# Sample attention of branches A and B: scores of block n + 1 and values of block n - 1 emitted as one task

## The chip, the cores and the metric

The kernel runs on one core of a Trainium2 chip. The metric is the device time of one execution in microseconds (us). The time before is 1967.59 us, the median of 3 runs (1961.37 to 1970.36).

The engines are named as in the profile: PE is TensorE's matrix multiply, PEld its weight load, DVE is VectorE, ACT is ScalarE, POOL is GpSimd, SP is SyncE, which here only issues DMAs.

## The reference, cut to what matters

One layer of a streaming encoder works on 1152 tokens: 1024 of a prompt and 8 samples of 16 new tokens each. Three attention branches are computed from one projection, each is multiplied by a gate, and their projections are summed; a feed-forward part follows.

```
x += W_o( sum_b sigmoid(gate_b(xn)) * P_b(branch_b(xn)) ),  xn = RMSNorm(x)
x += W_down( relu(RMSNorm(x) W_up)^2 )
```

The change touches the attention of the samples in branches A (band attention with a bias by distance) and B (forgetting attention). For each of the 8 samples, 16 queries of 8 heads read 512 cached keys and 16 new ones:

```
kk = jnp.concatenate([k_cache, k_new], axis=1)
vv = jnp.concatenate([v_cache, v_new], axis=1)
s = jnp.einsum('bqhd,bkhd->bhqk', q, kk).astype(jnp.float32) * (d ** -0.5)
s = s + rel_bias_lookup(rel_bias, dist)
p = jax.nn.softmax(s, axis=-1).astype(vv.dtype)
o = jnp.einsum('bhqk,bkhd->bqhd', p, vv)
```

## The kernel before, in words

**Stages.** After the projections come six attention stages, in this order: the prompt in branch A, the samples in A, the prompt in B, the samples in B, the prompt against the memory, the samples against the memory (`attend`, L1851). Then a rest of filler work, the output projection and the feed-forward part.

**What sets the order.** In the attention stages the order of the instructions is written by a planner, `Plan` (L58), while the program is built. It keeps modelled times of its own for each engine and each load. Its list of tasks is the stage's: scores, transposes, values and turns. Each task has a `ready` function, an `emit` function and the name of a chain; of one chain, tasks go in order, and a chain's first task that isn't ready holds the others of that chain back, though not those of another. `run` (L148) looks at up to 12 tasks and emits the first whose `ready` has passed. If there is none, `fill` (L135) emits one step of the filler instead: three matmuls of 128x384 with the result `z`. The filler is one stream for all stages, first the gates' products (`gates`, L948) and then the products of the merge (`merge`, L1005). The merge goes through the branches in the order A, B, memory, and through three thirds of the tokens. The planner's choice fixes each engine's order; on the chip each engine then goes through its instructions in that order and waits where data are late.

**The merge's operands.** A third of a branch's output is loaded in four quarters, each to a staging buffer `wst` (a ring of 3) and then split in a high and a low part, `hi` (`load`, L1043). For branch A a third may load once the last gate products of that third are emitted, for branch B once A's last merge product of that third is emitted.

**One sample in A and B** (`sample_ab`, L1509). A block n is one sample. Eight heads with 16 queries each fill 128 rows of scores as four groups of 32, so the scores (L1576) and the values (L1638) are matmuls on a 128x32 part of the array, placed by `tile_position`: 4 for the cached keys (`kd`) with 512 columns and 4 for the new keys (`kn`) with 16, and 20 with 128 columns for the values (`vd` and the new ones). After the scores, `soften` adds the bias and takes the maximum on DVE, then comes the exponential on ACT and the normalization on POOL or DVE (`exp_norm`). Five transposes (L1611) bring the weights into the form that the values need, ACT copies them to `spt`, the values follow, ACT copies the result to `of`, and a transpose of it (`turn`, L1662) ends the block. All transposes and the filler use the whole 128x128 array. The task loop (L1683) lists, per n: transposes of n - 1, scores of n, turn of n - 2, values of n - 1.

**The loads of a sample** are issued on SP's queue: keys (`kd`, 1 MB in A and B, a ring of 3, `KB`), values (`vd`, 1 MB, ring of 3) and, in B, a bias per block. Key n is issued once the scores of n - 3 are emitted, value n once the values of n - 3 are.

**The samples against the memory** (`sample_m`, L1693) are not touched by the change. They are 4 pairs of samples with keys and values of 512 KB (`kd<-in_cmk`, `vd<-in_cmv`) and the same steps; a score matmul there is 32x256. `queries` fills `qb`, which the scores read.

Most helpers' instructions carry line L203, all matmuls through the `pe` helper L215 and transposes L222.

Of the kernel before, what the change touches and what calls it, by code (L numbers as in the profile page):

```python
# [31 lines left out]
DB = 8  # L32
# [155 lines left out]
def tile_encoder(ctx: ExitStack, tc: tile.TileContext, i, o):  # L188
# [40 lines left out]
    def tl(pool, shape, dt=F32, tag=None, bufs=None):  # L229
        uid[0] += 1  # L230
        return pool.tile(list(shape), dt, tag=tag, name=f"{tag}_{uid[0]}", **({"bufs": bufs} if bufs else {}))
# [501 lines left out]
    for k in range(KD):  # L733
        n = {0: 1, 1: 1, 2: 1, 3: 1, 4: 2, 6: 2}.get(k)
# [270 lines left out]
    def merge(wpool, late):  # L1005
# [104 lines left out]
        for bi, (f, c) in ((bi, st) for bi in range(3) for st in steps):  # L1110
            x = 8 * bi + f
            for k in range(4):
                yield lambda: max(at["w", x], at["o", order[bi], c, k], plan.bank("z") if k == 0 else 0.0)
                if k == 0:
# [4 lines left out]
                    for y in {(4, 0): (2, 3), (5, 0): (3,), (6, 0): (), (7, 0): (), (7, 2): (2,)}.get((f, c), (2,) if c == 0 else ()):  # L1119
                        if x + y < 24:  # L1120
# [5 lines left out]
        late["h"] = lambda: (([[hi[c, kh] for kh in range(2)] for c in range(NC)],  # L1126
                              [[lo[c, f] for f in range(8)] for c in range(NC)]), order[2] == "m")

    def exp_norm(p, s, n, nm, pool, scale=-1.0, sm=None):

        sm = tl(pool, (P, 1), tag="sm", bufs=4)
        act.activation(p, s, AF.Exp, bias=nm, scale=scale, accum_out=sm)
        yield plan.op("act", n + 240)
        ri = tl(pool, (P, 1), tag="ri", bufs=4)
        vec.reciprocal(ri, sm)
        yield plan.op("vec", 8)
        k = plan.first(n, ("vec2", 0.3), ("gps1", 0))
        (vec if k == "vec2" else gps).tensor_scalar(p, p, ri, 1.0, ALU.mult, ALU.mult)
        yield plan.op(k, n)
# [369 lines left out]
    def sample_ab(b, pool):  # L1509
# [66 lines left out]
        def scores(n):  # L1576

            cols_ = (0, PAST), (PAST, DS)

            def soften(st):  # L1580
                yield plan.now + plan.LAT
                s = tl(pool, (P, NK), tag="s")
                bias, nm = biases[n if b == "b" else 0], None
                for (bk, ps), (x, hn) in zip(st, cols_):
                    m = tl(pool, (P, 1), tag="nm", bufs=4)
                    vec.tensor_tensor_reduce(s[:, x:x + hn], ps[:, :hn], bias[:, x:x + hn], -1.0,
                                             BIG if nm is None else nm, ALU.add, ALU.min, m)
                    t = plan.op("vec", hn)
                    plan.free(bk, t)
                    nm = m  # L1590
                at["m", n] = 0
                yield t
                yield from exp_norm(s, s, NK, nm, pool)
                ss_[n] = s
                at["p", n] = plan.t

            def ready():
                return max(at["k", n], at["q"], plan.bank("s"), 0 if n < 2 else at["t", n - 2])

            def emit():  # L1600
                st = []
                for x, hn in cols_:
                    st.append((plan.take("s"), tl(psum["s"], (P, 512), tag="s")))
                    for pr in range(4):
                        pe.matmul(st[-1][1][32 * pr:32 * pr + 32, :hn], qb[:, n, pr, :],
                                  kn[:, pr, n * DS:(n + 1) * DS] if x else kk[n][:, pr, :], start=True, stop=True, tile_position=(0, 32 * pr))
                at["s", n] = 0
                plan.spawn(soften(st))
            return [(ready, emit, ("s", n))]

        def transposes(n):  # L1611

# [25 lines left out]
        def values(n):  # L1638

            def ready():  # L1640
                return max(at["T", n, 512], at["T", n, P], at["V", n], plan.bank("tp"))

            def emit():
                bk = plan.take("tp")
                pv = tl(psum["tp"], (P, 512), tag="tp")
                for k in range(5):
                    for pr in range(4):
                        pe.matmul(pv[32 * pr:32 * pr + 32, 0:P], pts[n][k][:, 32 * pr:32 * pr + 32], vv[n][k][:, pr * P:(pr + 1) * P],
                                  start=k == 0, stop=k == 4, tile_position=(0, 32 * pr))
                at["v", n] = 0  # L1650
                plan.spawn(take(bk, pv[:, 0:P], n))
            return [(ready, emit, ("v", n))]

        def take(bk, pv, n):
            yield plan.now + plan.LAT
            of[n] = tl(pool, (P, P), tag="of")
            act.activation(of[n], pv, AF.Copy)
            t = plan.op("act", P)
            plan.free(bk, t)
            at["o", n] = t  # L1660
# [19 lines left out]

        plan.spawn(keys())
        plan.spawn(vals())
        for n in range(DB + 2):  # L1683
            if 0 <= n - 1 < DB:
                yield from transposes(n - 1)
            if n < DB:
                yield from scores(n)
            if 0 <= n - 2:
                yield from turn(n - 2)
            if 0 <= n - 1 < DB:  # L1690
                yield from values(n - 1)

    def sample_m(pool):  # L1693
# [165 lines left out]
    with tc.tile_pool(reuse_waits="tile", name="fg", bufs=1, side="right") as pool:  # L1859
        plan.spawn(forget_gates(pool))  # L1860
        attend("aa", lambda p: prompt_ab("a", p))
    attend("sa", lambda p: sample_ab("a", p))
    late["a"] = 0
    attend("ab", lambda p: prompt_ab("b", p))
# [451 lines left out]
```

## Time and profile before

| What | Value |
|---|---|
| profiled execution | 1967.87 us |
| its span | 1966.1 us |
| median of the runs shown | 1967.59 us (1961.37 to 1970.36) |
| mean granted clock of TensorE | 0.996 |
| samples in A, samples in B (about) | 566 to 645 us, 850 to 936 us |
| prompt against memory, samples against memory (about) | 936 to 1019 us, 1019 to 1066 us |

The profiled execution's own time is 0.28 us above the median of the runs, and its span is what the trace covers. A row of the timeline gives the start in us, the duration in us, the engine, the line, the operation, the tiles (out <- in), the part of the array or of the tile that it works on, its size, its type and the count of records merged in it; in brackets stands the idle time just before and what ended it. A matmul of full float32 on a part of the array shows two records, so four of them are x8; one of 128x384 shows one. A row of the windows gives start and end, length, then busy time and count for PE, PEld, DVE, ACT and POOL, the granted clock of TensorE as a share of full speed, the busy share of the DMA engines, and GB/s.

### The profile page before, as it was taken

The numbers are of one execution on the slowest core, as the hardware profiler recorded it, in microseconds if no ns is written. First come the engines' busy times: TensorE is split into PE (matmuls) and PEld (weight loads), VectorE is DVE, ScalarE is ACT, GpSimd is POOL, SyncE is SP. The second block draws the span as 40 slices with busy tenths as digits, with TensorE's granted clock in tenths as the row PEclk, the third lists the DMA queues.
The fourth block names the chain that finished last, engine by engine and source line by source line (L and its number), as shares of the span: only waits on it lengthen the run. The fifth ranks groups of instructions, "written<-read, shape, count | busy, mean of one in ns | idle before, by whom it ended". The sixth has DMA issues, their size and how long they took to land. (4 is left out here: it accounts for less than half of the span.)

```text
span 1966.1 us, 33787 instructions
## 1 busy us (share of the span) xinstructions
PE 1931.2 (98%) x12338; PEld 1704.0 (87%) x12338; DVE 1210.7 (62%) x2305; ACT 947.8 (48%) x1846; POOL 531.5 (27%) x575
## 2 busy tenths in 40 slices
PE   9999999999999999999999999999999999999999
PEld 9887888788888888888998987899999997888887
DVE  7866657675633555523675824975565565785775
ACT  7645556556643556533452314554444453543332
POOL 4243433342210334211133101254445430000000
PEclk9999999999999999999999999999999999999999
DMA  8456454743267433188667442054343459563463
GB/s 279 159 160 183 122 169 150 251 124 105 84 207 277 158 107 101 62 280 293 196 223 267 150 163 97 22 198 151 132 144 125 141 190 325 174 204 96 134 194 127
DMA packets 203812, 330.52 MB, mean 168 GB/s; under 512 B 29285, under 2 KB 101622, under 8 KB 199550
## 3 DMA queue, kind: packets, MB, share of 16 engines
q1 hardware_dynamic: 146504, 270.44, 42.2%
q10 hardware_dynamic: 57142, 57.93, 8.9%
q8 instruction: 97, 1.59, 0.3%
q14 instruction: 69, 0.57, 0.1%
HBM read 243.11 MB, written 85.18 MB: 167 GB/s over the span
## 5 line engine op out<-in xcount | busy, mean ns | idle before, releaser
L1912 PE MATMUL b<-r 128*128 128x512 f32 (+2 forms) x2200 | 456.5, 356 | 4.7 <-ACT r L203 2.7
L1912 PEld LDWEIGHTS b<-r 128*128 128x128 f32 x2200 | 378.9, 189 | 62.7 <-ACT r L203 3.6
L203 ACT ACTIVATE r<-fa 128x512 fp32r<-128x512 f32 (+4 forms) x264 | 213.0, 816 | 336.3 <-PE b L1912 284.3
L203 DVE TENSOR_TENSOR r<-fa,r 128x512 fp32r<-128x512 f32 (+4 forms) x264 | 268.2, 1028 | 145.3 <-ACT r L203 138.8
L215 PE MATMUL z<-hi,whi 128*128 128x384 f32 x960 | 313.4, 359 | 2.7 <-DVE tg L203 2.6
L1912 PE MATMUL b<-r,r 128*128 128x320 f32 (+1 forms) x1928 | 287.8, 299 | 5.7 <-DVE r L203 5.6
L1912 PEld LDWEIGHTS b<-r,r 128*128 128x128 f32 x1928 | 271.0, 190 | 7.4 <-DVE r L203 7.4
L215 PE MATMUL z<-hi,wlo 128*128 128x384 f32 x768 | 259.6, 338 | 0.0
L203 POOL TENSOR_TENSOR fa<-fa 128x512 f32<-128x512 f32 x114 | 173.3, 1528 | 225.0 <-ACT fa L203 125.8
L215 PE MATMUL z<-wa,hi 128*128 128x512 f32 (+1 forms) x732 | 199.4, 359 | 5.8 <-ACT wa L203 2.8
L215 PE MATMUL z<-lo,whi 128*128 128x384 f32 x576 | 194.9, 338 | 0.0
L215 PEld LDWEIGHTS z<-hi,whi 128*128 128x128 f32 x960 | 177.3, 189 | 16.7 <-issue 8.0
L203 ACT ACTIVATE s<-s,nm 128x256 f32<-128x256 f32 (+8 forms) x180 | 121.2, 679 | 63.8 <-DVE nm L203 61.0
L215 PEld LDWEIGHTS z<-wa,hi 128*128 128x128 f32 x732 | 126.3, 188 | 25.4 <-ACT wa L203 3.6
L215 PEld LDWEIGHTS z<-hi,wlo 128*128 128x128 f32 x768 | 145.0, 189 | 0.0
L203 POOL TENSOR_SCALAR s<-s,ri 128x256 f32<-128x256 f32 (+7 forms) x107 | 73.7, 693 | 232.2 <-DVE ri L203 223.6
L215 PE MATMUL z<-wa,lo 128*128 128x512 f32 (+1 forms) x366 | 129.0, 354 | 0.0
L203 DVE CUSTOM_DVE_ANT_0 s<-s,bias 128x384 f32<-128x384 f32 (+3 forms) x144 | 74.5, 555 | 88.0 <-PE s L215 87.2
L215 PEld LDWEIGHTS z<-lo,whi 128*128 128x128 f32 x576 | 109.7, 190 | 0.0
L203 DVE TENSOR_TENSOR fa<-b,fa 128x256 f32<-128x256 f32 (+1 forms) x160 | 71.6, 452 | 58.7 <-PE b L1912 52.0
L222 PE MATMUL tp<-ident,s 128*128 128x128 f32 (+1 forms) x680 | 105.7, 277 | 1.2 <-POOL s L203 1.1
L203 ACT ACTIVATE pt<-tp 128x256 f32<-128x256 f32 (+3 forms) x153 | 65.4, 449 | 85.1 <-PE tp L222 79.7
(229 smaller groups left out, 3129.8 us busy)
## 6 DMA issues: line engine op xcount, KB each, us to landing
td<-fa SPq DMA_DIRECT2D x112, 256.0 KB, 2.1
rw<-in_w_in SPq DMA_DIRECT2D x96, 256.0 KB, 3.2
fa<-td SPq DMA_DIRECT2D x80, 256.0 KB, 2.7
fa<-in_w_down SPq DMA_DIRECT2D x76, 256.0 KB, 3.1
fa<-in_w_up SPq DMA_DIRECT2D x32, 512.0 KB, 4.1
tg<-tg ACTq DMA_DIRECT2D x72, 192.0 KB, 2.6
th<-tg SPq DMA_DIRECT2D x72, 192.0 KB, 3.0
wst<-in_w_g ACTq DMA_DIRECT2D x48, 256.0 KB, 3.2
```

Of the source, the lines that this page charges most:

```text
L203: ins = f(*a, **k)
L215: ins = nc.tensor.matmul(out, lhsT, rhs, **k)
L222: ins = nc.tensor.transpose(*a)
L1912: pin(nc.tensor.matmul(ps, lh, rh, **k))
```

## The change

A new function `joined` takes the scores of block n + 1 and the values of block n - 1 and makes one task of them. Its `ready` is the later of both, and its `emit` calls both, the scores first. All score tasks now have the same chain name, `"s"`, in place of one per block, so that joined tasks go in order. The loop lists the scores of blocks 0 and 1 first and then, per n: transposes of n - 1, turn of n - 2, the joined task; the last two blocks' values stand alone. That makes 6 joined tasks in each of A and B. Matmuls, transposes, copies and loads are the same as before in number and size; what moves is their order, in these two stages and, since the planner's modelled times go on from there, in the stages behind them.

```diff
+    def joined(scores, values):
+        if values is None:
+            return scores
+        (r0, e0, chain), (r1, e1, _) = scores, values
+        def emit():
+            e0()
+            e1()
+        return lambda: max(r0(), r1()), emit, chain
...
-            return [(ready, emit, ("s", n))]
+            return [(ready, emit, "s")]
...
         plan.spawn(keys())
         plan.spawn(vals())
-        for n in range(DB + 2):
-            if 0 <= n - 1 < DB:
+        yield from scores(0)
+        yield from scores(1)
+        for n in range(1, DB + 2):
+            if n - 1 < DB:
                 yield from transposes(n - 1)
-            if n < DB:
-                yield from scores(n)
             if 0 <= n - 2:
                 yield from turn(n - 2)
-            if 0 <= n - 1 < DB:
+            if n + 1 < DB:
+                yield joined(*scores(n + 1), *values(n - 1))
+            elif n - 1 < DB:
                 yield from values(n - 1)
```

**Place 1: PE, the samples in A, about the fourth block.** Tiles are named as in the rows: `s` are scores (from keys `kd` or new keys `kn` and queries `qb`), `tp<-vd,spt` are values, `tp<-ident,s` and `tp<-ident,of` transposes, `z` the filler. Before:

```order
L215 MATMUL z_6663<-hi_154_222,wlo_6408 128x384
L215 MATMUL s_6725<-kd_6502,qb_6319 32x512 x4
L215 MATMUL s_6730<-kn_6317,qb_6319 32x16 x4
L215 MATMUL z_6663<-hi_154_222,whi_6407 128x384
L215 MATMUL z_6663<-lo_162_230,whi_6407 128x384
...
L215 MATMUL tp_6748<-vd_6378,spt_6707 32x128 x16
L215 MATMUL tp_6748<-v_1156_6324,t_1152_6320 32x128 x4
L222 MATMUL tp_6777<-ident_203,s_6699 128x128 x4
```

With the change:

```order
L215 MATMUL z_6723<-hi_163_231,wlo_6383 128x384
L215 MATMUL s_6744<-kd_6502,qb_6319 32x512 x4
L215 MATMUL s_6749<-kn_6317,qb_6319 32x16 x4
L215 MATMUL tp_6754<-vd_6378,spt_6704 32x128 x16
L215 MATMUL tp_6754<-v_1156_6324,t_1152_6320 32x128 x4
L222 MATMUL tp_6787<-ident_203,s_6699 128x128 x4
```

Three filler matmuls that stood between the scores and the values stand elsewhere now. Over the whole program, a stretch of PE's order on 32-wide parts of the array, with full-array work on both sides, occurs 10 times in A where it was 15, 9 in B where it was 10, and 7 in the samples against the memory where it was 6.

**Place 2: PE, the end of the samples in B and the start of the prompt against the memory.** The rows `z<-hi,wlo` with `lo` beside them are the last gate products; the first row with a new `hi` after them are merge products. The products of `z_10894` before, of `z_10906` with the change, are the first of the last third of branch A's operand. Before, from the last gate product on:

```order
L215 MATMUL z_10729<-hi_164_232,wlo_10319 128x384
L215 MATMUL z_10808<-hi_2055_10439,whi_10395 128x384
...
L215 MATMUL tp_10838<-vd_10483,spt_10764 32x128 x16
L215 MATMUL tp_10838<-v_1927_9781,t_1925_9779 32x128 x4
...
L215 MATMUL z_10867<-hi_2093_10631,whi_10395 128x384
...
L222 MATMUL tp_10879<-ident_203,of_10865 128x128
...
L215 MATMUL z_10894<-hi_2119_10776,whi_10395 128x384
```

With the change:

```order
L222 MATMUL tp_10791<-ident_203,of_10781 128x128
...
L215 MATMUL z_10741<-hi_164_232,wlo_10324 128x384
L215 MATMUL z_10848<-hi_2065_10467,whi_10378 128x384
...
L215 MATMUL z_10882<-hi_2102_10681,whi_10378 128x384
...
L215 MATMUL z_10906<-hi_2122_10805,whi_10378 128x384
```

In both there are 24 filler matmuls between the last gate product and the last third. The last values of branch B's samples and the turn that followed them stood in between, and now stand ahead of the last gate product.

**Place 3: PE and SP, the samples against the memory, from the first scores on.** `kd` and `vd` are the memory's keys and values here. PE before:

```order
L215 MATMUL s_12015<-kd_11918,qb_11915 32x256 x4
L215 MATMUL s_12015<-kd_11939,qb_11915 32x256 x4
...
L222 MATMUL tp_12071<-ident_203,s_12041 128x128 x2
...
L215 MATMUL s_12092<-kd_11960,qb_11915 32x256 x4
L215 MATMUL s_12092<-kd_11984,qb_11915 32x256 x4
L215 MATMUL tp_12102<-vd_11925,spt_12070 32x128 x8
L215 MATMUL tp_12102<-vd_11949,spt_12070 32x128 x8
...
L222 MATMUL tp_12154<-ident_203,of_12132 128x128 x2
```

PE with the change:

```order
L215 MATMUL s_11923<-kd_11854,qb_11822 32x256 x4
L215 MATMUL z_11945<-hi_2393_11857,whi_11472 128x384
...
L222 MATMUL tp_11958<-ident_203,s_11942 128x128 x2
...
L215 MATMUL tp_11965<-vd_11843,spt_11957 32x128 x8
L215 MATMUL tp_11965<-vd_11875,spt_11957 32x128 x8
L222 MATMUL tp_11988<-ident_203,of_11986 128x128 x2
L215 MATMUL s_11993<-kd_11888,qb_11822 32x256 x4
L215 MATMUL s_11993<-kd_11911,qb_11822 32x256 x4
L222 MATMUL tp_12015<-ident_203,s_12008 128x128 x2
L215 MATMUL tp_12021<-vd_11902,spt_12014 32x128 x8
```

SP's queue with the change, in the same place (before, no `wst` stood between the keys and values here):

```order
L203 DMA kd_11825<-in_cmk 128x1024
L203 DMA vd_11843<-in_cmv 128x1024
L203 DMA th_11849<-tg_76 128x384
L203 DMA kd_11854<-in_cmk 128x1024
L203 DMA wst_11859<-oTb_72 128x384
L203 DMA wst_11868<-oTb_72 128x384
L203 DMA vd_11875<-in_cmv 128x1024
L203 DMA wst_11877<-oTb_72 128x384
...
L203 DMA kd_11888<-in_cmk 128x1024
```

Before, 24 filler matmuls stand between the first scores and their transposes, 9 between these and the next scores and 12 between the first values and their turn. With the change the first scores are followed by 6 filler matmuls up to their transposes and 3 more up to the first values, and from these on, through turn, second scores, second transposes and second values, by none. The filler's next product there, `z_11945`, is the one that reads the operand which the three `wst` loads fill. Between the last matmul of the prompt against the memory and the first scores stand 57 filler matmuls before and 51 with the change.

## The prediction

> **What bounds the kernel now.** First the page's head and its busy times:
>
> ```profile
> span 1966.1 us, 33787 instructions
> PE 1931.2 (98%) x12338; PEld 1704.0 (87%) x12338; DVE 1210.7 (62%) x2305; ACT 947.8 (48%) x1846; POOL 531.5 (27%) x575
> ```
>
> PE works 98% of the span, no other engine over 62%, so the time is PE's work plus the few places where PE waits. Then the windows of the stages concerned, in order the samples in A, the samples in B, the prompt against the memory, the samples against the memory:
>
> ```profile
> 566.00:636.00 70.00, 70.00 (x750) 59.22 (x749) 23.09 (x75) 25.70 (x61) 5.64 (x8) 1.00 0.75 281
> 850.00:936.00 86.00, 82.81 (x819) 72.85 (x818) 27.40 (x82) 30.60 (x72) 11.66 (x19) 0.98 0.88 305
> 936.00:1019.00 83.00, 82.85 (x511) 79.44 (x511) 60.85 (x111) 45.20 (x123) 20.57 (x17) 1.00 0.60 185
> 1019.00:1066.00 47.00, 46.07 (x410) 41.05 (x409) 23.16 (x50) 10.25 (x26) 9.59 (x11) 1.00 0.84 299
> ```
>
> In A PE never waits. In B it is idle for 86.00 - 82.81 = 3.19 us, at a DMA share of 0.88; the two memory stages lose 0.15 and 0.93 us. So the change can win only what a matmul on a part of the array costs beyond its own work and 3 us of waits in B; it can lose more wherever it leaves PE without filler. The waits in B, from PE's timeline, and the window behind the longest:
>
> ```profile
> 863.19 1.06 PE L215 MATMUL s<-kd,qb 128*32 128x512 f32 x8 [0.22 <-DMA kd<-in_cbk]
> 894.69 1.07 PE L215 MATMUL s<-kd,qb 128*32 128x512 f32 x8 [0.96 <-DMA kd<-in_cbk]
> 909.30 0.33 PE L222 MATMUL tp<-ident,of 128*128 128x128 f32 x1 [1.90 <-ACT of L203]
> 910.50:913.90 3.40, 3.40 (x15) 3.23 (x14) 0.01 (x1) 0.40 (x1) 0.72 (x2) 0.51 0.87 335
> ```
>
> Twice the scores wait for keys and once a turn waits for ACT's copy of its values, 0.22 + 0.96 + 1.90 = 3.08 us. After the 1.90 us the granted clock is 0.51 for 3.40 us, which costs 3.40 x 0.49 = 1.7 us more, though PE counts as busy.
>
> **Part 1, fewer visits to a part of the array.** What one costs is read in A, where nothing waits: scores alone, values alone, and a place where both already stand together, each with the filler at its sides.
>
> ```profile
> 596.16 0.34 PE L215 MATMUL z<-hi,wlo 128*128 128x384 f32 x1
> 596.43 1.07 PE L215 MATMUL s<-kd,qb 128*32 128x512 f32 x8
> 597.75 0.34 PE L215 MATMUL z<-lo,whi 128*128 128x384 f32 x1
> ...
> 582.46 0.34 PE L215 MATMUL z<-hi,wlo 128*128 128x384 f32 x1
> 582.73 1.08 PE L215 MATMUL tp<-vd,spt 128*32 128x128 f32 x32
> 584.24 0.34 PE L215 MATMUL z<-lo,whi 128*128 128x384 f32 x1
> ...
> 611.64 0.33 PE L215 MATMUL z<-hi,wlo 128*128 128x384 f32 x1
> 611.90 1.08 PE L215 MATMUL tp<-vd,spt 128*32 128x128 f32 x32
> 613.02 1.04 PE L215 MATMUL s<-kd,qb 128*32 128x512 f32 x8
> 614.32 0.34 PE L215 MATMUL z<-lo,whi 128*128 128x384 f32 x1
> ```
>
> From filler to filler it is 597.75 - 596.16 = 1.59 us around scores, 1.78 around values, 2.68 around both. One filler matmul takes 0.18 of each (three start in 0.53 us, row below), so apart it is 1.41 + 1.60 = 3.01, together 2.50: about 0.5 with all neighbours out, but the filler ahead and behind is itself drawn out by the visit, and counting two spacings (0.35) out, 1.59 + 1.78 - 0.35 - 2.68 = 0.34. I take 0.34; the bounds are 0.34 and 0.5. The order shows 26 visits where there were 31, not 12 fewer, since several already stood together: 5 x 0.34 = **-1.7 us** (bounds -1.7 and -2.5). [...]
>
> **Part 2, samples in A.** The joined task asks for the keys of block n + 1 while the values of n - 1 are due, so keys are needed a few us earlier than when they could drift. The stage has no wait to lose or give back, and filler on both sides: **0**, bounds 0 and +2 (two key waits of B's larger size, 0.96).
>
> **Part 3, samples in B.** Joined, a score whose keys are late holds the values behind it on PE, and with them ACT's `of`, the turn, and the ring slot for the next values. On the other side `of` gets more room, since the turn stands behind more work. I keep the two key waits at two or three times their size, 0.22 + 0.96 to about 3.5, and let the 1.90 and its slow clock go: 3.5 - 4.8 = **-1.3 us**. Bounds: all of it gone, -4.8; a wait of 0.96 at each of the 6 joined tasks on top of what is there and one slow stretch, about +4 net.
>
> **Part 4, start of the prompt against the memory.** After the last gate product PE goes on with merge products of branch A, whose last third is only loaded once that gate product is emitted:
>
> ```profile
> 932.63 0.34 PE L215 MATMUL z<-hi,wlo 128*128 128x384 f32 x1
> 940.85 0.45 PE L215 MATMUL z<-hi,whi 128*128 128x384 f32 x1 [0.15 <-DVE hi L203]
> ```
>
> It takes 940.85 - 932.63 = 8.22 us to the last quarter of that operand, and PE had 0.15 us to wait. With the change the last values and the turn stand ahead of the gate product; 34 matmuls at 0.177 are left, 6.0 us. The load path is the same length, so PE waits 2.2 instead of 0.15: **+2.0 us**. Bounds 0 (the loads are faster with the queue emptier) and +4 (this stage's own keys in their way).
>
> **Part 5, samples against the memory.** This stage isn't edited, but loses its cover: the filler's next product reads an operand whose loads stand between the keys and values on SP's queue, so the planner puts little filler there. Rows of PE, SP, DVE, POOL and ACT before:
>
> ```profile
> 1019.10 0.34 PE L215 MATMUL z<-hi,wlo 128*128 128x384 f32 x1
> 1019.63 0.34 PE L215 MATMUL z<-hi,wlo 128*128 128x384 f32 x1
> 1018.95 0.46 SPq L203 DMA_DIRECT2D kd<-in_cmk  x1
> 1021.64 0.65 SPq L203 DMA_DIRECT2D kd<-in_cmk  x1
> 1030.27 0.33 SPq L203 DMA_DIRECT2D kd<-in_cmk  x1
> 1028.91 0.64 PE L215 MATMUL s<-kd,qb 128*32 128x256 f32 x8
> 1029.87 0.64 PE L215 MATMUL s<-kd,qb 128*32 128x256 f32 x8 [0.32 <-DMA kd<-in_cmk]
> 1034.71 0.38 PE L222 MATMUL tp<-ident,s 128*128 128x128 f32 x2
> 1035.13 0.39 ACT L203 ACTIVATE spt<-tp 128x256 f32<-128x256 f32 x1 [3.47 <-PE tp L222]
> 1037.48 1.06 PE L215 MATMUL tp<-vd,spt 128*32 128x128 f32 x32
> 1037.73 0.43 DVE L203 TENSOR_REDUCE nm<-s 128x1 f32<-128x256 f32 x1 [0.34 <-PE s L215]
> 1039.05 0.48 POOL L203 TENSOR_SCALAR s<-s,ri 128x256 f32<-128x256 f32 x1 [0.80 <-DVE ri L203]
> 1038.65 0.37 ACT L203 ACTIVATE of<-tp 128x256 f32<-128x256 f32 x1
> th<-tg SPq DMA_DIRECT2D x14, 192.0 KB, 6.5
> ```
>
> The durations: three fillers 0.53; keys landed 1029.87 - 1021.64 = 8.2 after their issue, which is 10.9 after the first key's; softmax from the scores' end to POOL's end 1039.53 - 1037.73 = 1.80; transposes to the end of `spt` 0.81; values to the end of `of` 1039.02 - 1037.48 = 1.54. Walk along the new order from the first key's issue at t = 0. 51 fillers take 9.0; first scores at 8.9 to 9.5, their second half waits for its keys until 10.9: **1.4**. Scores end at 11.6, six fillers reach 12.6, softmax is done at 13.4: **0.7**. Transposes to 13.7, three fillers to 14.3, values to 15.3, `of` at 15.8: **0.5**. Turn to 16.2, half of the second scores to 16.8, then the fourth keys: issued 11.3 after the first, landed 6.5 (as the smaller `th`, last row) to 8.2 later, t = 17.8 to 19.5; I take 18.7: **1.9**. Scores end at 19.4 and transposes follow at once, softmax in full: **1.8**. The values behind them wait for `spt`: **0.4**. Together 6.7, less the 0.93 of before: **+5.8 us**. Filler left out here stands later, so no work goes, and all the waits count. Bounds: without the two key waits 3.4 - 0.9 = +2.5; these doubled +9.1.
>
> **Part 6, the clock behind new gaps.** A gap of 1.90 cost 1.7 us of slow clock (above). But one of 2.07 us did not:
>
> ```profile
> 422.56 0.28 PE L222 MATMUL tp<-ident,lf 128*72 128x128 f32 x1 [2.07 <-DVE lf L203]
> 423.00:427.00 4.00, 4.00 (x33) 3.66 (x33) 3.96 (x17) 3.52 (x10) 0.80 (x1) 1.00 0.43 105
> ```
>
> New gaps near that size are three: 2.0 in part 4, 1.9 and 1.8 in part 5. I take two slow stretches of 3.40 us, **+3.4 us**; bounds 0 and 7 (four, as the small gaps of part 5 stand close). What follows all of this, the rest of the filler, the output projection and the feed-forward part, keeps its work and its order: **0**.
>
> **Sum**, against the profiled 1967.87: -1.7 + 0 - 1.3 + 2.0 + 5.8 + 3.4 = +8.2, so **1976.1 us**. That execution lies 0.28 above the median of the runs, so the change is +0.4%. A measurement of this kernel can't tell 0.5%, 9.8 us, from nothing; the bounds are then 1957.8 and 1977.4.
>
> **Rivals.** *The starved stage at half clock.* If PE stays at the slow clock from the first scores against the memory to the second values, its work there, scores 2.5, fillers 1.6, transposes and turn 1.1, values 2.1, 7.3 in all, costs 7.3 / 0.51 - 7.3 = 7.0 us more, and with part 4's stretch 1.7: 8.7 for the 3.4. Sum +13.5, **1981.4 us**, slower. For it: five waits in some 14 us, and a slow stretch lasts 3.40. Against: the waits are short, and the slow clock fills some of them. It decides when the clock costs over 5.0, three stretches.
>
> *No slow clock at all.* The 2.07 us gap speaks for it, the 1.90 us one against. Without the 3.4, +4.8: **1972.7 us**. [...]
>
> *Loads in time.* SP's order brings keys earlier, B's waits vanish (-4.8), part 4 falls to 0 and part 5 to +2.5 without slow clock: -1.7 - 4.8 + 2.5 = -4.0, **1963.9 us**. Against: the DMA share of 0.88 and 0.84 leaves little room.
>
> *Only the joins count*, if PE's waits stay as they were everywhere: -1.7, **1966.2 us**. Against: the filler is gone from the rows of part 5.
>
> **How the numbers follow.** Forecast (one to three slow stretches, 1971 to 1978) 0.37, of it 0.06 over 1977.4; half clock 0.33; none 0.15; loads in time 0.08; only joins 0.04; something faster by over 0.5%, for which I find no mechanism, 0.03. So faster 0.03, same 0.31 + 0.15 + 0.08 + 0.04 = 0.58, slower 0.06 + 0.33 = 0.39. The range 1965 to 1987 leaves out most of the loads-in-time case at its lower end, and above it part 5's upper bound (9.1 for 5.8) on top of the half clock, 1984.7, with 2 to spare; the likeliest case's own is 1971 to 1978.
>
> **What would show it.** Windows of the same stages: A with no wait and 5 visits fewer; B with under 3.5 us idle and no gap of 1.90 before a turn; the first `z` of A's last third waiting about 2 us for DVE's `hi`; in the samples against the memory five waits, for keys, softmax, `of`, keys, softmax, near 6.7 us together, and a granted clock under 0.9 there. Wrong, if that stage has under 3 us idle, or B's waits grow past 5.

## The result, and the profile after

The changed kernel takes 1987.47 us, the median of 5 runs (1984.31 to 1988.34), against 1967.4 us of the kernel before (5 runs, 1961.37 to 1970.36): a ratio of 1.0107, 95% interval 1.0094 to 1.0121. The change costs about 20 us, clear of noise. The prediction was 1976.1 us, in a range up to 1987.0, with no difference as the likeliest verdict; the measured time lies just above the range, on the side of its first rival.

The head of the page, the profiled execution being 1988.34 us:

```profile
span 1986.5 us, 33788 instructions
PE 1938.9 (98%) x12338; PEld 1708.7 (86%) x12338; DVE 1217.2 (61%) x2308; ACT 947.8 (48%) x1846; POOL 532.2 (27%) x572
```

The span is 20.4 us longer (1986.5 against 1966.1). Of these, 12.7 us are PE's idle time (1986.5 - 1938.9 = 47.6, before 34.9) and 7.7 us are busy time of the same instructions, so PE ran slower for a while (the granted clock is 0.96 and 0.89 in the last two rows below). The windows of the same stages as before (samples in A, samples in B, prompt against the memory, samples against the memory):

```profile
566.00:636.00 70.00, 70.00 (x746) 60.17 (x746) 22.82 (x73) 25.26 (x61) 5.67 (x8) 1.00 0.78 288
850.00:936.00 86.00, 81.21 (x820) 71.38 (x819) 28.71 (x85) 30.58 (x72) 8.21 (x16) 1.00 0.91 302
936.00:1019.00 83.00, 79.22 (x471) 74.69 (x470) 55.54 (x102) 43.22 (x116) 16.12 (x13) 0.96 0.55 168
1019.00:1066.00 47.00, 38.93 (x339) 30.98 (x338) 17.62 (x41) 11.68 (x30) 7.87 (x9) 0.89 0.79 278
```

The next table gives PE's idle time in us, and beside it what the granted clock costs (length x (1 - clock), read stretch by stretch):

| Stage | idle before | idle after | slow clock before | slow clock after | difference |
|---|---|---|---|---|---|
| samples in A | 0 | 0 | 0 | 0 | 0 |
| samples in B | 3.19 | 4.79 | 1.7 | 0 | -0.1 |
| prompt against the memory | 0.15 | 3.78 | 0 | 3.4 | +7.0 |
| samples against the memory | 0.93 | 8.07 | 0 | 5.1 | +12.2 |

The two stages that the change edits cost what they did, with more idle time in B and no slow clock. The two that it doesn't edit lose 19.2 us. The filler shows why these two: from the first scores of the samples in B to their last turn PE does 303 filler matmuls before and 276 after, and in the samples against the memory 141 before and 75 after. Here is this starved stage in PE's timeline, each row with a wait from the first scores on, and then ACT's rows that belong to it:

```profile
1029.38 0.64 PE L215 MATMUL s<-kd,qb 128*32 128x256 f32 x8 [1.13 <-DMA kd<-in_cmk]
1031.10 0.44 PE L215 MATMUL z<-hi,whi 128*128 128x384 f32 x1 [1.08 <-ACT hi L203]
1032.17 0.44 PE L215 MATMUL z<-hi,whi 128*128 128x384 f32 x1 [0.64 <-POOL hi L203]
1037.42 0.44 PE L222 MATMUL tp<-ident,of 128*128 128x128 f32 x2 [0.51 <-ACT of L203]
1039.16 0.64 PE L215 MATMUL s<-kd,qb 128*32 128x256 f32 x8 [0.72 <-DMA kd<-in_cmk]
1041.71 0.44 PE L222 MATMUL tp<-ident,s 128*128 128x128 f32 x2 [1.92 <-POOL s L203]
1044.22 1.94 PE L215 MATMUL tp<-vd,spt 128*32 128x128 f32 x32 [2.08 <-ACT spt L203]
```

```profile
1043.38 0.52 ACT L203 ACTIVATE hi<-wst 128x384 fp32r<-128x384 f32 x1 [2.49 <-DMA wst<-oTb]
1043.81 0.36 ACT L203 ACTIVATE spt<-tp 128x256 f32<-128x256 f32 x1
```

The waits sum to 8.08 us. Five of the seven were forecast (keys, `of`, keys, softmax, `spt`), though `spt` at 0.4 and not 2.08. The two of the filler for `hi` were not. ACT shows why `spt` is late: in ACT's order the copy of the operand's last quarter, `hi<-wst`, stands ahead of it and waits until 1043.38 us for its own transfer, while the transposes that `spt` copies had ended at 1042.15. The next rows are the start of the prompt against the memory: the last gate product, and the waits for the last third of branch A's operand.

```profile
935.37 0.33 PE L215 MATMUL z<-hi,wlo 128*128 128x384 f32 x1
940.97 0.44 PE L215 MATMUL z<-hi,whi 128*128 128x384 f32 x1 [0.42 <-DVE hi L203]
943.38 0.44 PE L215 MATMUL z<-hi,whi 128*128 128x384 f32 x1 [1.80 <-ACT hi L203]
943.97 0.46 PE L215 MATMUL z<-hi,whi 128*128 128x384 f32 x1 [0.15 <-DVE hi L203]
945.43 1.28 PE L215 MATMUL z<-hi,whi 128*128 128x384 f32 x2 [0.68 <-ACT hi L203]
```

0.42 + 1.80 + 0.15 + 0.68 = 3.05 us where 2.2 were forecast. From the last gate product to the operand's last quarter it is 945.43 - 935.37 = 10.06 us, against 8.22 before. The stage's other 0.73 us are one wait for its softmax. The slow clock behind both stages' waits is read from windows of 3.41 us, laid on the edges of the slow stretches: first at the start of the prompt against the memory, then in the samples against the memory, and last an earlier place of the same execution:

```profile
940.85:944.27 3.42, 1.35 (x5) 0.78 (x5) 1.23 (x3) 0.52 (x1) 0.00 (x0) 1.00 0.93 292
944.27:947.68 3.41, 2.73 (x8) 1.94 (x7) 1.17 (x3) 1.04 (x2) 0.00 (x0) 0.50 0.68 233
947.68:951.09 3.41, 3.41 (x12) 3.41 (x12) 1.42 (x3) 1.15 (x2) 0.00 (x0) 0.50 0.48 138
951.09:954.51 3.42, 3.42 (x23) 3.42 (x22) 1.53 (x3) 0.00 (x0) 0.00 (x0) 1.00 0.55 181
...
1029.60:1033.01 3.41, 1.70 (x14) 1.00 (x6) 1.05 (x3) 1.50 (x4) 1.16 (x2) 1.00 1.03 362
1033.01:1036.43 3.42, 3.42 (x31) 2.12 (x33) 0.56 (x1) 0.91 (x2) 0.32 (x1) 0.50 0.98 352
1036.43:1039.84 3.41, 2.13 (x34) 0.73 (x26) 0.35 (x2) 0.38 (x1) 0.00 (x0) 1.00 1.02 394
1039.84:1043.25 3.41, 0.44 (x2) 0.20 (x2) 0.59 (x2) 0.56 (x2) 0.48 (x1) 1.00 1.04 418
1043.25:1046.67 3.42, 2.45 (x34) 1.97 (x35) 0.56 (x1) 1.24 (x4) 0.00 (x0) 0.50 1.00 373
1046.67:1050.08 3.41, 3.41 (x22) 1.80 (x20) 1.16 (x2) 0.46 (x1) 1.38 (x1) 0.50 0.96 365
1050.08:1053.49 3.41, 3.41 (x24) 3.33 (x21) 1.83 (x6) 0.56 (x2) 0.57 (x1) 1.00 0.74 232
...
422.03:425.44 3.41, 1.56 (x16) 0.88 (x14) 3.07 (x13) 0.38 (x1) 0.79 (x1) 1.00 0.27 84
425.44:428.85 3.41, 3.19 (x24) 2.97 (x25) 3.41 (x15) 2.73 (x7) 0.81 (x1) 1.00 0.38 83
```

In the two memory stages three stretches had PE busy for 1.35, 1.70 and 0.44 of 3.41 us, and the clock of the next was 0.50 each time. The slow stretches with PE busy for 2.73 and 2.45 us were each followed by another at 0.50. Behind the one with 2.13 us the clock was 1.00, and at 422.03 us it was 1.00 behind 1.56 us too, so PE's busy time in one stretch doesn't by itself tell the clock of the next.

### The profile page after: what moved, and what is told of

The parts are those of the page before. It is cut to its first block, busy times and chain, and to the rows that moved or that the text cites. A ratio compares the mean times of both kernels' runs of the same rounds, so it can differ in the third digit from the quotient of the medians.

```text
span 1986.5 us, 33788 instructions
## 1 busy us (share of the span) xinstructions
PE 1938.9 (98%) x12338; PEld 1708.7 (86%) x12338; DVE 1217.2 (61%) x2308; ACT 947.8 (48%) x1846; POOL 532.2 (27%) x572
## 5 line engine op out<-in xcount | busy, mean ns | idle before, releaser
L203 POOL TENSOR_SCALAR s<-s,ri 128x256 f32<-128x256 f32 (+8 forms) x107 | 73.8, 695 | 253.7 <-DVE ri L203 247.0
L203 ACT ACTIVATE pt<-tp 128x512 f32<-128x512 f32 (+3 forms) x153 | 65.3, 448 | 83.2 <-PE tp L222 76.9
```

The source lines that it names most:

```text
L203: ins = f(*a, **k)
```

## The experiments

**Theory 1**: the joined tasks cost nothing where they stand; the samples in B emit fewer filler matmuls, so the filler stream arrives later at its change from one branch's operand to the next, and this falls into the memory stages, where it takes PE's cover away. **Theory 2**: the joined task costs by itself. **Theory 3**: slow stretches that any new order brings. Every ratio is to the kernel before on the same chip, which had medians of 1964.32, 1963.91 and 1964.64 us beside the three groups of runs; it compares all runs of the two kernels and need not equal the quotient of the medians. The times in the expectations go by the first result's 1967.4 us, some 3 us more, so ratios are the better comparison.

**Only A joined.** Branch B keeps its old loop and chains.

```diff
-            return [(ready, emit, "s")]
+            return [(ready, emit, "s" if b == "a" else ("s", n))]
...
+        if b == "a":
+            yield from scores(0)
+            yield from scores(1)
...
+        else:
+            for n in range(DB + 2):
+                if 0 <= n - 1 < DB:
+                    yield from transposes(n - 1)
...
```

> Only the samples of branch A have the joined task; B keeps one task each for scores and values. The planner's order from the samples in B on, with both memory stages, is then that of the kernel before. Theory 1 (the loss comes from the two memory stages, which lose their filler because less filler is emitted in B): no loss, 5 visits of 0.34 us less than before, so 1.7 us under it, about 1965.7 us (1962 to 1970), and both memory stages idle for under 1.5 us together. Theory 2 (the joined task itself costs: values held behind late keys, in both branches alike): about half of the 20 us, 1977 us. Theory 3 (slow stretches of the clock that any new order brings by chance): 1970 to 1975, with at least two more slow stretches somewhere.

Measured: 1964.38 us, ratio 0.9993 (0.9982 to 1.0004), the memory stages idle for 0.00 and 0.80 us. No loss, and 303 and 141 filler matmuls in the two stages, as before. The gain of 1.7 us for 5 visits would be 0.9991; the interval holds it, and no gain as well.

**Only B joined**, the same edit with `"b"`.

> Only the samples of branch B have the joined task. The order of both memory stages is then the one with the whole change. Theory 1: all of the loss, about 1987 to 1989 us (the changed kernel's 1987.5, and up to 1.7 more for A's visits), with 3 to 4 us idle in the prompt against the memory and 7 to 8 us idle in the samples against the memory. Theory 2: 1977 us if both branches share the loss. Theory 3: anything from 1970 to 1990, with the idle time of the memory stages no higher than 1.5 us.

Measured: 1988.11 us, ratio 1.0113 (1.0098 to 1.0129): all of the loss, with 83.00 - 78.66 = 4.34 and 47.00 - 38.81 = 8.19 us idle in the memory stages and a granted clock of 0.96 and 0.85. The filler counts are those of the whole change, 276 and 75:

```profile
936.00:1019.00 83.00, 78.66 (x470) 74.06 (x469) 55.53 (x103) 43.74 (x117) 16.81 (x14) 0.96 0.53 164
1019.00:1066.00 47.00, 38.81 (x340) 32.12 (x339) 17.20 (x41) 10.01 (x26) 8.70 (x10) 0.85 0.80 282
```

**The whole change with early thirds.** The merge's order of steps is changed, so that the last third of a new operand is first read 48 and not 24 matmuls after the change of branch.

```diff
-        steps = [(f, c) for f in range(5) for c in range(NC)] + [(f, c) for c in range(NC) for f in range(5, 8)]
+        steps = [(f, c) for c in range(NC) for f in range(2)] + [(f, c) for f in range(2, 5) for c in range(NC)] + [(f, c) for c in range(NC) for f in range(5, 8)]
```

> The whole change, and the merge takes its first two output blocks for one third of the tokens after the other (two blocks of the first third, two of the second, two of the third, then as before), so that 48 filler matmuls in place of 24 stand between the end of one branch and the first use of the next branch's last third. The joined tasks stay as they are. Theory 1: the idle time and slow clock of the two memory stages go (7.0 and 12.2 us over the kernel before in the profile), so 1987.5 - 19.2 = about 1968 us (1963 to 1971), with under 0.5 us idle in the prompt against the memory and under 1.5 in the samples against the memory. Theory 2: the joined tasks are still there, so 1985 to 1988. Theory 3: no forecast but a spread of 5 us.

Measured: 1963.81 us, ratio 0.9998 (0.9986 to 1.0009). The joined tasks are all there and the 20 us are gone, in the two stages named. The samples in B still emit only 276 filler matmuls, but the samples against the memory have 144:

```profile
936.00:1019.00 83.00, 82.85 (x513) 79.71 (x511) 59.83 (x112) 44.89 (x120) 19.14 (x16) 1.00 0.59 186
1019.00:1066.00 47.00, 47.00 (x419) 42.46 (x419) 24.64 (x53) 10.11 (x26) 6.79 (x9) 1.00 0.84 304
```

**Filler first.** Between the samples in B and the prompt against the memory the planner catches up with the filler.

```diff
     late["b"] = 0
+    for _ in range(24):
+        plan.advance()
+        plan.fill()
     attend("am", prompt_m)
```

> The whole change, but between the samples in B and the prompt against the memory the planner emits filler until none is ready by its own times (some 22 steps). The order of the samples against the memory is then that of the kernel before, row for row in kind; the wait for the last third of branch A's operand at the start of the prompt against the memory stays. Theory 1: the 12.2 us of the samples against the memory go, the 7.0 at the start of the prompt against the memory stay: about 1975 us (1970 to 1979). Theory 2: 1985 to 1988. Theory 3: no forecast but a spread of 5 us.

Measured: 1970.61 us, ratio 1.0036 (1.0021 to 1.0051). The samples against the memory are cured (1.09 us idle from 1019 to 1066 us, full clock; the stage itself runs from 1036 to 1073 us here), the start of the prompt against the memory isn't (3.06 us idle, clock 0.98). The forecast of 1975 us is +7.6 over 1967.4; measured is +6.3. So about 7 per mille, 14 us, of the loss were the samples against the memory, and the rest, 7 us, the stage ahead of it, near the table's 12.2 and 7.0. The profiled execution, 1977.06 us, is the slowest of the seven; it loses 5.1 us of slow clock in B besides.

**Early thirds alone**, on the kernel before, with the same line of `steps`.

> The kernel before (no joined task) with the merge's first two output blocks taken one third of the tokens after the other, as in the run with early thirds. Theory 1 (the change loses only by the filler it takes from the memory stages): without the joined task there was hardly anything to cure (0.15 + 0.93 us idle in both memory stages), so 0 to 1 us under the kernel before, and 0 to 2 us over the joined kernel with early thirds: what the saved visits are worth. Theory 2 (joined tasks cost, early thirds gain as much by themselves): 10 to 20 us under the kernel before.

Measured: 1969.15 us, ratio 1.0022 (1.0009 to 1.0034), slower than expected by either theory. The memory stages have 1.07 and 0 us idle, so there was nothing to cure, but the filler behind them waits for the gates (`th`) and the memory's operand (`om`), 3.88 us in the stretch from 1066 to 1110 us, where the kernel before has 0.82:

```profile
1066.00:1110.00 44.00, 40.12 (x248) 37.86 (x247) 35.98 (x60) 17.88 (x35) 11.38 (x9) 1.00 0.53 161
```

With the same merge order, the joined kernel is thus at 0.9998 and the one without joins at 1.0022, some 2.4 per mille or 5 us apart, more than the saved visits (1.7 us) would give. In the traces 3.1 us of it lie in this stretch (3.88 us idle against 0.76). The run also shows that the early thirds don't gain by themselves, so that Theory 2 can't be saved by them.

**Warm.** The whole change, with 16 transposes more that keep PE busy in its two longest waits of the samples against the memory; a transposed identity is written to a bank that the next real instruction overwrites. The question is whether the slow clock behind these waits stays.

```diff
                 t = tl(psum["tp"], (P, 2, P), tag="tp")
+                for _ in range(8 if n == 1 else 0):
+                    tc.keep_in_program_order(nc.tensor.transpose(t[:, 0, :], ident, ident))
...
                 pv = tl(psum["tp"], (P, 2, P), tag="tp")
+                for _ in range(8 if n == 1 else 0):
+                    tc.keep_in_program_order(nc.tensor.transpose(pv[:, 0, :], ident, ident))
```

> The whole change, with 16 transposes of the identity more in the samples against the memory, 8 ahead of the second block's transposes and 8 ahead of its values, into the bank that these overwrite. PE then works through most of the two longest waits there (1.92 and 2.08 us), all else is the same order. [...]

Measured: 1983.69 us, ratio 1.0097 (1.0077 to 1.0116). The first two windows hold the end of the first wait for keys and the filler's two waits, the last two the two waits that were filled:

```profile
1026.52:1029.93 3.41, 1.08 (x9) 0.37 (x9) 1.04 (x2) 1.39 (x4) 0.98 (x1) 1.00 1.00 377
1029.93:1033.35 3.42, 3.35 (x14) 2.81 (x18) 1.06 (x3) 0.91 (x2) 0.50 (x2) 0.50 0.96 332
...
1036.76:1040.17 3.41, 2.52 (x26) 1.93 (x18) 0.59 (x2) 0.56 (x2) 0.48 (x1) 1.00 1.02 404
1040.17:1043.59 3.42, 2.42 (x40) 1.81 (x38) 0.97 (x2) 1.70 (x4) 0.00 (x0) 1.00 1.04 406
```

The stretch that was busy for 0.44 us of 3.41 is now busy for 2.4 to 2.5, and no slow stretch follows; the stretch whose waits weren't filled (1.08 busy) is still followed by one, at 0.50. The stage's slow clock fell from 5.1 to 1.7 us. In the time 3.4 us are 1.7 per mille; measured is 1.0 less than the whole change. The interval holds both the whole change's 1.0107 and the 1.0090 that is 1.7 per mille less, so the time neither shows nor excludes the gain.

**No operand.** The whole change in the same order, with branch B's last third neither loaded nor split; its products read the second third's tiles.

```diff
-                    sp.dma_start(st, src[:, k, :])
+                    if (b, c) != ("b", 2):
+                        sp.dma_start(st, src[:, k, :])
...
+            if (b, c) == ("b", 2):
+                yield plan.op("act", CH)
+                e = plan.first(CH, ("vec", 0.5), ("gps", 0))
+                plan.give(w)
+                yield plan.op(e, CH)
+            else:
...
-                    lambda _: tuple(w[:, k, :] for w in op[order[bi], c]), 1, k == 0, k == 3)
+                    lambda _: tuple(w[:, k, :] for w in op[order[bi], 1 if (order[bi], c) == ("b", 2) else c]), 1, k == 0, k == 3)
```

> The whole change in the same order on PE, but the last third of branch B's operand is neither loaded nor split: its products read the second third's tiles (that part of the merge is computed from wrong data). Left out are four loads of 192 KB on SP's queue and four copies on ACT with four subtractions. Theory 1a (in the samples against the memory the operand itself is half of the loss: its loads in the keys' way on SP's queue, its copies ahead of the softmax and of the weights' copy on ACT, and the filler that waits for it): the filler's waits (1.72 us) go, the values' 2.08 falls to 0.4, the keys' 1.85 to under 1, one slow stretch goes: 8.1 us idle there become 3 to 4.5, and the time 1980 to 1983 us. Theory 1b (only the filler that is missing from the order counts, the keys and softmax chain are as long without the operand): 6.5 us or more idle there, 1985 to 1987 us.

Measured: 1979.99 us, ratio 1.0088 (1.0071 to 1.0105), 47.00 - 40.64 = 6.36 us idle in the samples against the memory, slow clock 3.4 in place of 5.1. Its waits there:

```profile
1024.41 0.64 PE L215 MATMUL s<-kd,qb 128*32 128x256 f32 x8 [0.28 <-DMA kd<-in_cmk]
1027.92 0.64 PE L215 MATMUL s<-kd,qb 128*32 128x256 f32 x8 [2.87 <-DMA kd<-in_cmk]
1030.61 0.69 PE L222 MATMUL tp<-ident,s 128*128 128x128 f32 x2 [0.30 <-POOL s L203]
1033.90 0.44 PE L222 MATMUL tp<-ident,of 128*128 128x128 f32 x2 [0.51 <-ACT of L203]
1037.25 0.44 PE L222 MATMUL tp<-ident,s 128*128 128x128 f32 x2 [1.91 <-POOL s L203]
1038.16 1.08 PE L215 MATMUL tp<-vd,spt 128*32 128x128 f32 x32 [0.47 <-ACT spt L203]
```

As expected by 1a, the filler's waits are gone and `spt` fell from 2.08 to 0.47, which, with ACT's rows above, shows the operand's copy ahead of it as its cause. Against 1a, the idle time is 6.4 and not 3 to 4.5, since the first scores now wait 0.28 and 2.87 us for keys and the softmax costs 1.91 as before. So 1b is nearer, in idle time and in the ratio (its 1985 us are 1.0089, the upper end of 1a 1.0079): most of the stage's loss is the filler that is missing. The operand's loads and copies add 3.4 us in this pair of traces, 1.7 of idle time and 1.7 of clock.

**No join, filler held.** The kernel before, without any joined task; in the samples in B 6 steps of filler go unused.

```diff
...
     def fill(self):
+        if self.hold and self.now > self.hold_at:
+            self.hold -= 1
+            self.now += 0.53
+            return True
...
+    plan.hold, plan.hold_at = 6, 470
     attend("sb", lambda p: sample_ab("b", p))
+    plan.hold = 0
```

> The kernel before, without any joined task, but in the samples in B the planner lets 6 steps of filler (18 matmuls, 3.2 us) go unused: its own time passes and nothing is emitted. The filler is then as far behind as with the change, and the planner's order of the samples against the memory is the one with the change (6, 3 and 0 filler matmuls between its steps). Theory 1 (the change loses because its stage B emits less filler, whatever the reason, so that the end of branch A's products falls into the samples against the memory): up to 3 us idle in B, 6 to 8 us idle in the samples against the memory, 3 to 7 us of slow clock in the memory stages, ratio to the kernel before 1.009 to 1.012. Theory 2 (it needs the joined tasks themselves): ratio 1.000 to 1.002, from the 3 us held back.

Measured: 1986.27 us, ratio 1.0101 (1.0077 to 1.0126), without one joined task. The samples in B have 273 filler matmuls, and the samples against the memory have 75, in the very order of the changed kernel. B is idle for 86.00 - 81.81 = 4.19 us, more than the 3 expected. These are its memory stages (83.00 - 78.69 = 4.31 and 47.00 - 40.72 = 6.28 us idle) and the waits for softmax and `spt`:

```profile
936.00:1019.00 83.00, 78.69 (x474) 74.34 (x473) 55.51 (x102) 44.04 (x118) 17.11 (x15) 0.98 0.54 169
1019.00:1066.00 47.00, 40.72 (x358) 33.92 (x357) 20.24 (x46) 11.79 (x30) 10.12 (x11) 0.93 0.82 295
```

```profile
1035.17 0.44 PE L227 MATMUL tp<-ident,s 128*128 128x128 f32 x2 [1.92 <-POOL s L208]
1037.43 1.94 PE L220 MATMUL tp<-vd,spt 128*32 128x128 f32 x32 [1.83 <-ACT spt L208]
```

These waits, those of the filler for `hi` (1.33 and 0.63 us) and that for `of` (0.51) come at the same places as with the change; only the two waits for keys don't. The runs of this kernel spread from 1977.22 to 1988.4 us, and the profiled one is the fastest, with 5.1 us of slow clock in the memory stages where the changed kernel had 8.5. Theory 2 is excluded: the loss comes without the joined task, and the joined task comes without the loss. Theory 3 is too: A joined and early thirds are new orders as well, and lose nothing.

**Early thirds for branch A's products alone**, the whole change otherwise.

```diff
+        early = [(f, c) for c in range(NC) for f in range(2)] + [(f, c) for f in range(2, 5) for c in range(NC)] + steps[15:]
...
-        for bi, (f, c) in ((bi, st) for bi in range(3) for st in steps):
+        for bi, (f, c) in ((bi, st) for bi in range(3) for st in (early if bi in (0,) else steps)):
```

> The whole change with early thirds in branch A's part of the merge alone. This cures the start of the prompt against the memory; the end of A's products then falls ahead of the samples against the memory, since the planner no longer lets time pass at the start. Theory 1: no filler is missing in either stage (9, 12 and 12 matmuls stand where the change has 6, 3 and 0), so the ratio is that of the run with all early thirds, 0.999 to 1.001, with under 2 us idle in both stages together. Theory 2: 1.008 or more.

Measured: 1965.32 us, ratio 1.0001 (0.9986 to 1.0015), 0.11 and 1.08 us idle in the memory stages. Both memory stages are cured, though only the merge's first part was changed: the end of A's products now falls ahead of the samples against the memory, which have 138 filler matmuls.

**Late weights.** In every run with the planner's old landing times, a turn in the samples in B waits 1.1 to 2.8 us for ACT's `of`. ACT's rows of the changed kernel show a weight's split ahead of it, `whi<-wr`, that waited for its transfer:

```profile
907.44 0.63 ACT L203 ACTIVATE whi<-wr 128x512 fp32r<-128x512 f32 x1 [2.32 <-DMA wr<-in_w_pa]
907.98 0.26 ACT L203 ACTIVATE of<-tp 128x128 f32<-128x128 f32 x1
```

The planner is told that the merge's weights land 4 us later, first with the whole change and early thirds, for all weights:

```diff
-                raw[x] = st, w, plan.load(256, "dma2")
+                raw[x] = st, w, plan.load(256, "dma2") + 4.0
```

> The whole change with early thirds, and the planner takes the merge's weights to land 4 us later than its model says, so that on ACT the copy of a block's values in the samples in B stands ahead of the first two weight splits and not behind them. The turn that waits 1.1 to 2.8 us for that copy in all runs so far then waits for under 0.5, and the slow clock behind it (1.7 us in most) goes. If the copy is late because of the weight's transfer ahead of it on ACT: 2 to 4 us under the run with early thirds, 0.998 of the kernel before. If it is late for another reason (the values themselves): no difference.

Measured: 1970.18 us, ratio 1.0028 (1.0016 to 1.0041). The turn waits no more, and there is no slow stretch in B; but five waits for keys take its place in B (86.00 - 82.27 = 3.73 us idle, with early thirds alone 3.06), the memory stages are idle for 1.14 and 1.33 us where they were for 0.15 and 0, and behind them PE waits 1.94 us for `th`. A wait of 2.13 us for `whi` further on is no loss against early thirds, where it is 2.15 (last row):

```profile
1078.26 0.58 PE L215 MATMUL z<-om,whi 128*128 128x384 f32 x2 [1.94 <-DVE th L203]
...
1184.13 0.50 PE L1925 MATMUL b<-whi,hi 128*128 128x512 f32 x1 [2.13 <-ACT whi L203]
...
1180.08 0.50 PE L1925 MATMUL b<-whi,hi 128*128 128x512 f32 x1 [2.15 <-ACT whi L203]
```

The cause of the turn's wait was right and the gain wasn't there: other waits grew, and why isn't shown. So one more run takes the 4 us for the first two weights alone (`+ (4.0 if x < 2 else 0.0)`), on the kernel that has only A joined.

> The joined task in the samples in A alone, and the first two weights of the merge are taken to land 4 us later by the planner; the orders of PE in both memory stages stay those of the kernel before, and on ACT the copy of a block's values in B stands ahead of the first two weight splits. If the gap of 1.8 to 1.9 us ahead of a turn in B and the slow stretch behind it (1.7 us) go and nothing takes their place: 2 to 3.6 us under the run with A alone, ratio 0.9975 to 0.9985. If, as in the run with all merge weights late, key waits take their place: 0.999 to 1.000.

Measured: 1961.37 us, ratio 0.9981 (0.9969 to 0.9994), faster than both kernels. Against the run with A alone (0.9982 to 1.0004) the intervals overlap, so the step from there isn't resolved. In the trace the turn's wait is gone; in B 1.58 us are idle, with A alone 4.07, and the clock is full:

```profile
850.00:936.00 86.00, 84.42 (x834) 73.86 (x833) 30.77 (x90) 31.51 (x74) 11.30 (x19) 1.00 0.94 319
```

## Why the prediction was wrong, point by point

**What bounds the kernel** was right, and so was the place: the loss is in the two stages that the change doesn't edit, and the runs with B alone, with early thirds and with the filler held show it from three sides. Of the signs named, the waits in the samples against the memory came (8.1 us for 6.7) and so did a clock under 0.9 there (0.89). What failed are sizes, above all of part 6, and with them the choice between the forecast and its first rival.

- **Part 1, visits**, -1.7: not excluded, not shown. With A alone 0.9993 (0.9982 to 1.0004) against the 0.9991 that the same -1.7 would be. PE's busy time less what slow stretches add to it (half of the time that PE is busy in them, by their clock of 0.50) is 1924.5 us before, 1922.7 with A alone and 1924.7 with the whole change, so the profiles don't settle it.
- **Part 2, samples in A**, 0: right, no wait.
- **Part 3, samples in B**, -1.3: -0.1 in the profile. The key waits came out near their size (2.8 for 3.5, in five waits), but the turn's wait for `of`, which was to go, stayed at 1.98: its cause was not the turn's place on PE but a weight's transfer ahead of `of` on ACT, which this change doesn't move. Its slow clock went all the same: in the two stretches of 3.41 us from 903.30 us on, which hold the 1.98, PE was busy for 3.00 and 1.83 us, and behind them the clock was 1.00. Why isn't shown.
- **Part 4, start of the prompt against the memory**, +2.0: +3.6 of idle time, of which 2.9 are the forecast wait (3.05 less the 0.15 of before). The step "the load path is the same length" was wrong: 10.06 us for 8.22.
- **Part 5, samples against the memory**, +5.8: +7.1. Three steps of the walk came out at 1.1, 0.5 and 1.9 for 1.4, 0.5 and 1.8; the second keys cost 0.7 for 1.9. Missed was that the filler left in that stage waits for its own operand (1.7), which hides the first softmax (0.7), and that the operand's copy stands ahead of `spt` on ACT (2.08 for 0.4). The loads on SP's queue were followed, their copies on ACT were not.
- **Part 6, slow clock**, +3.4: this is the step that failed. The new stages have 3.4 + 5.1 = 8.5 us. A price of 1.7 was put on each gap of about 1.9 us, with two gaps taken. In this execution the waits of 1.08 and 0.64 us, none of that size, left PE busy for 1.70 us of one stretch of 3.41, and the clock of the next was 0.50; and twice a slow stretch, with PE busy for 2.73 and 2.45 us, was followed by a second one, so that one place cost 3.4. In the run with added transposes PE was busy for 2.52 and 2.42 us in the stretches of the filled waits, and no slow one followed. What sets when one starts isn't shown.

The table's three differences, -0.1 + 7.0 + 12.2, make 19.1 of the span's 20.4 us, against +8.2 forecast. Of the 10.9 us between them the clock is 5.1, part 4 1.6, part 5 1.3 and part 3 1.2; the other 1.7 are the visits, whose gain would not be in this table and isn't seen in the busy time either. The table counts 0.8 us twice, where PE waits inside a slow stretch. The rest is elsewhere: the profiled execution has 4.5 us more idle time and slow clock in its first 400 us (17.2 against 12.7), though both kernels have the same order there, and some 2 us less behind the memory stages. The other traces have 8.7 to 13.5 us in those first 400 us; why this one has 17.2 isn't shown.

The rival of half clock, 1981.4 us, put 8.7 us on the slow clock, and 8.5 came. Its size was right and its course was not quite: the clock was full from 1036.43 to 1043.25 us in between, and the start of the prompt had two slow stretches, not one. What it lacked are the other terms, which it shared with the forecast.

The verdict follows: chances of 0.58 for no difference and 0.39 for slower were the wrong way round, since the clock was a term of five stretches and was put at two.

## What to carry to other kernels

An edit in a list scheduler's input is priced at the places where the filler changes its operand, not where the edit stands: count how many filler matmuls the edited stage emits, and look where the stream's next load has to land. On each engine, look for what stands ahead in program order and waits for a transfer, for an ACT copy behind a late split makes the chain wait for the split's transfer (here 2.08 us, and 0.47 without it). Telling the planner of the later landing of two weights, with A joined, gave 0.9981, where A joined alone gave 0.9993; the turn's wait went, but the two intervals overlap.

## What the runs showed of the hardware

In the changed kernel's trace the clock was 0.50 in stretches of 3.41 us. The ones at 944.27 and 1033.01 us lie 26 x 3.413 us apart, the ones at 67.04 and 1292.42 us 359 x 3.413. In its two memory stages the stretches with PE busy for 1.35, 1.70 and 0.44 us of 3.41 were followed by a slow one and the one with 2.13 was not, and after a slow stretch with PE busy for 2.45 or 2.73 came a second one. Other places went otherwise: at 422.03 us of the same execution the clock stayed at 1.00 behind 1.56 us busy, and in the kernel before it was 1.00 from 423 to 427 us, behind the wait of 2.07 us ahead of 422.56 us. With early thirds for A alone, a slow stretch at 878.37 us with PE busy for 2.76 was followed by full speed (1.00 from 882 to 890 us). What decides between these cases isn't shown; one place cost 1.7 or 3.4 us here. Of the runs with the filler held, the fastest, 1977.22 us, has a mean granted clock of 0.997, the other five (1983 to 1988 us) 0.990 to 0.992. Where in those five the clock was slow isn't shown.
